# A recurrence whose gate products move behind the next group's second product

## The chip, the cores and the metric

One Trainium2 chip, one of its cores. The metric is device time in microseconds of one execution of the whole program. Engines are named as in the profile: PE (TensorE, matmuls; PEld its weight loads), DVE (VectorE), ACT (ScalarE), POOL (GpSimd), and SP (SyncE), which issues nearly all DMAs in order.

## What is computed

One inference step of a two-layer decoder: a recurrent layer (Hawk/Griffin RG-LRU) and a forgetting-attention layer, for a prompt of 2048 tokens and for 8 x 8 sample tokens, with a model width of 1024. The change lies in the recurrent layer alone:

```
def rg_lru(u, h0, w_ga, b_ga, w_gx, b_gx, lam):
    ub = uf.reshape(B, T, N_RNN_BLOCKS, RNN_BLOCK)
    r = sigmoid(einsum('btnc,ncd->btnd', ub, w_ga) + b_ga)
    i = sigmoid(einsum('btnc,ncd->btnd', ub, w_gx) + b_gx)
    log_a = -RGLRU_C * r * softplus(-lam)
    a = exp(log_a)
    inp = sqrt(-expm1(2.0 * log_a)) * (i * uf)
    # h[t] = a[t] * h[t-1] + inp[t]

def recurrent_mixer(x, h0, conv_buf, w_in, conv_w, conv_b, w_ga, b_ga, w_gx, b_gx, lam, w_out):
    z = x @ w_in
    u, g = z[..., :D_RNN], z[..., D_RNN:]
    u, new_buf = causal_conv(u, conv_buf, conv_w, conv_b)
    h, h_last = rg_lru(u, h0, w_ga, b_ga, w_gx, b_gx, lam)
    return (h * silu(g)) @ w_out, h_last, new_buf
```

Two products per channel block, u and g, come from the input; u is convolved over time, goes through two small gate products (128 x 128 per block), gives the decay a and the input of a scan over time, and the scan's result, times silu(g), is multiplied by w_out.

## The kernel before

**Tiling.** The tokens run through the recurrent layer in two chunks of 1024 (chunk 0 has the 64 sample tokens as well), here called phase 0 and phase 1 of the recurrence. In each, `phase_a1` (L588) loops over the eight channel blocks n (128 channels each) and, within a block, over three groups of tokens: 320, 384 and 384 columns in phase 0 (the 64 sample columns are in the first), 384, 384 and 256 in phase 1. A group is written (n, gi) below. Every product is taken in three float32r parts (`mm3`, L387 to L389: high x high, high x low, low x high), so u and g of a group are 24 matmuls each and its two gates 3 each.

**One group.** `u` is the first product (24 matmuls into a PSUM tile). ACT copies it to `up` (L710). `front` (L592) forms the convolution `uc` in four DVE passes (L597, three times L599), its rounded copy `uh` on POOL (L106) and the rest `ul` on DVE (L111). `gates` (L617) multiplies uh and ul by the block's gate weights gh and gl into two PSUM tiles and takes tanh on ACT (`tr`, `ti`, L624). `g` is the second product, and `tg` its silu in two steps (ACT tanh L724, DVE L725). `decay` (L629) makes `a`, a second tanh of tr and a square `w` on ACT (L635 to L637), then ti and w on DVE (L638, L639). When all three groups of a block are through, `decayed` (L671) takes one square root over the block (L681, with a table load before and after it); for the last block the root is taken group by group (L677). `scan` (L642) multiplies ti by w on POOL, scans over time on DVE (L653, the eight sample rows by short scans L649), carries the last state to the next group on POOL (`hcar`), multiplies by tg on POOL, rounds the result on ACT (`oh`) and DVE (`ol`), and stores both by DMA (L662, L663).

**Software pipelining.** A group's gates and decay are not done in its own turn but in the next group's: `pend` holds the group before. In the kernel before, a turn issues u, then the gates of pend, then g, then the decay of pend, then tg, then one waiting scan. The last group's gates follow the loop (L743).

**What sets the order.** The program is recorded in the order of the code, and a scheduler then places the instructions of each engine by that order's priority and by a timeline of its own, so that small pieces can be moved. Each engine then runs its list strictly in the order placed. Buffers: four PSUM tiles for u, g and y (`mm`), two for gates and transposes (`tp`); uc has three buffers, uh and ul two, tr two, ti and a four, w two, tg five.

**Around the phase.** `then()` and `begin()` (L740, L742) open `phase_a2` (L767), which multiplies oh and ol, read back from DRAM as `ohT` and `olT` (L781), by w_out into `y`; its first two token tiles are loaded in two halves (blocks 0 to 3 and 4 to 7). w_out comes in eight pieces through the staging buffer `wst` (L487, three buffers) and is split on ACT and DVE into high and low parts (`wh`/`wl`, then `woh4` to `woh7`). After phase_a2 of phase 0 come the attention layer's projections and part of the decoding for the samples, then phase 1, and then the rest.

Of the kernel before, what the change touches and what calls it, by code (L numbers as in the profile page):

```python
# [90 lines left out]
def tile_hawk_fox(  # L91
# [496 lines left out]
    def phase_a1(s, xs, a0, covered, feed, wk, out, then, begin, beside):  # L588
# [96 lines left out]
        for n in range(KB):  # L685
            W = feed.take()
            gst = wk.tile([P, 2, P], F32, name="gst", tag="gst")
            S.dma_start(gst[:, 0, :], a_w_ga[0, n])
            asked = S.dma_start(gst[:, 1, :], a_w_gx[0, n])
            gh = wk.tile([P, 2, P], F32R, name="gh", tag="gh", bufs=2)  # L690
            gl = wk.tile([P, 2, P], F32R, name="gl", tag="gl", bufs=2)
            cp(G, gh[:, :, :], gst[:, :, :])
            tt(G, gl[:, :, :], gst[:, :, :], f(gh[:, :, :]), ALU.subtract)
            for gi, (c0, C) in enumerate(s.groups):
                while covered < c0 + C:
                    covered = next(a0)
                so = sm if c0 == 0 else 0
                tn = C - so
                xh, xl = xs[gi]
                rh, rl = (lambda k: xh[:, k, :]), (lambda k: xl[:, k, :])  # L700
                up = wk.tile([P, 3 + mh], F32, name="up", tag="up", bufs=2)
                cp(G, up[:, 0:3], halo[:, n, :])
                ups = mmp("u")
                mm3(ups[:, :C], W.h(0, P), W.l(0, P), rh, rl, KB)
                us = None
                if so:
                    us = wk.tile([P, DB, 3 + DS], F32, name="us", tag="us")
                    cp(G, us[:, :, 0:3], gv[:, n, 11:35].rearrange("p (b j) -> p b j", b=DB))
                    A.copy(us[:, :, 3:], ups[:, :sm].rearrange("p (b q) -> p b q", b=DB))
                A.copy(up[:, 3:3 + tn], ups[:, so:C])  # L710
                uc, uh, ul = front(n, c0, C, ups, us, up, W)
                if so and n == 0:
                    decays()
                if beside and gi < 2:
                    with tc.issue_after(asked.ins):
                        beside.pop(0)()
                if pend:
                    trti = gated()
                gps = mmp("g")
                mm3(gps[:, :C], W.h(P, 2 * P), W.l(P, 2 * P), rh, rl, KB)  # L720
                if pend:
                    decayed(*trti)
                tg = wk.tile([P, mh], F32, name="tg", tag="tg", bufs=5)
                A.activation(tg[:, :C], gps[:, :C], AF.Tanh, scale=0.5)  # L724
                V.scalar_tensor_tensor(tg[:, :C], tg[:, :C], 1.0, gps[:, :C], op0=ALU.add, op1=ALU.mult)  # L725
                if scans:
                    scan(*scans.pop(0))
                pend = (n, c0, C, uc, uh, ul, tg, gh, gl)
                if n == KB - 1:
                    if gi == 0:  # L730
                        out.fetch()
                        out.fetch()
                    else:
                        out.split(min(gi, 2))
                elif gi == 0:
                    feed.fetch()
                    feed.fetch()
                else:
                    feed.split()
# [1275 lines left out]
```

## Time and profile before

| what | us |
|---|---|
| median of 3 runs | 2928.73 (2923.12 to 2936.70) |
| profiled execution | 2919.81 |
| its span | 2918.1 |
| PE busy | 2747.1 (94% of the span) |
| DVE busy | 1828.1 (63%) |
| ACT busy | 1267.6 (43%) |
| POOL busy | 1098.0 (38%) |
| first to last product of u, phase 0 | 32.8 to about 259 |
| phase 1 ends with the store of the last group | about 1126 |

Times in rows of the trace are microseconds from the start of the span. A row of the timeline reads: start, duration, engine, line, operation, tile written <- tiles read, shape, count, and in brackets how long the engine stood idle before it and what ended that. A row of a stretch reads: from:to, length, then busy time and instructions of PE, PEld, DVE, ACT and POOL, the granted clock of PE as a share, the share of the DMA engines and GB/s. A row of the waits reads: engine, tile and line that waited <- engine, tile and line waited for, microseconds in total, times, the longest. Matmuls overlap: the shown duration of one is longer than the step from one start to the next.

### The profile page before, as it was taken

What the parts mean: (1) busy time and instruction counts of PE and PEld (TensorE: products, weight loads), DVE (VectorE), ACT (ScalarE), POOL (GpSimd) and SP (SyncE); (2) the same over time, 40 slices, a digit from 0 to 9 for tenths busy, and PEclk for the clock granted to TensorE, in tenths of its full rate; (3) what the DMA queues carried; (4) which work ended last, traced back from release to release, by engine and by line L of the source; (5) the groups of instructions that cost most, each with busy time, mean ns of one, the idle gap of its engine ahead of it and who ended that gap; (6) DMA issues with size and microseconds to landing.
All of it is one profiled execution on the core that took longest, in us unless ns stands there. A gap on an engine that the chain in (4) does not pass through costs nothing.

```text
span 2918.1 us, 59421 instructions
## 1 busy us (share of the span) xinstructions
PE 2747.1 (94%) x21086; PEld 2224.8 (76%) x21086; DVE 1828.1 (63%) x3971; ACT 1267.6 (43%) x2874; POOL 1098.0 (38%) x1207
## 2 busy tenths in 40 slices
PE   5998999999998999999999999999999999999998
PEld 5997789988898997887888766565666665666787
DVE  7877457244256775676565676767677766655465
ACT  4656342222234665533334345444444544455221
POOL 1654110000003652100001265756565655659554
PEclk9999999999999999999999999999999999999999
DMA  4224536789745536689999978778788777862454
GB/s 127 80 86 125 169 124 188 203 243 300 224 142 177 178 107 191 215 303 325 341 314 333 338 261 293 239 255 277 253 271 269 255 259 240 284 222 61 131 184 131
DMA packets 484789, 636.03 MB, mean 218 GB/s; under 512 B 100888, under 2 KB 293145, under 8 KB 477276
## 3 DMA queue, kind: packets, MB, share of 16 engines
q1 hardware_dynamic: 484204, 630.13, 66.6%
q8 instruction: 167, 2.74, 0.4%
q0 software_dynamic: 288, 2.10, 0.3%
q14 instruction: 130, 1.06, 0.1%
HBM read 512.78 MB, written 133.85 MB: 222 GB/s over the span
## 4 chain that ended last, share of the span: by engine, by line
PE 55%; DMA 9%; DVE 7%; ACT 4%; SPq 3%; issue 2%; POOL 1%; DVEq 0%; ACTq 0%; POOLq 0%
PE ops L1675 8%; PE st L1651 5%; PE sx L1438 4%; PE st L1652 4%; PE dS L1202 3%; PE dO L1290 3%; PE y L389 3%; PE y L387 3%; PE y L388 3%; DMA raw<-in_cache_k_dram 2%; PE kv L387 2%; PE kv L389 2%; PE kv L388 2%; PE qg L387 2%; PE qg L389 2%
## 5 line engine op out<-in xcount | busy, mean ns | idle before, releaser
L1218 DVE STREAM_TRANSPOSE ktr<-raw 128x1024 f32<-128x1024 f32 x256 | 308.0, 1225 | 97.6 <-DMA raw<-in_cache_k_dram 73.5
L1440 DVE TENSOR_REDUCE mxs<-sx 128x1 f32<-128x512 f32 x384 | 253.8, 680 | 157.6 <-PE sx L1438 156.8
L387 PE MATMUL kv<-wh,xh 128*128 128x256 f32 (+3 forms) x1088 | 307.7, 287 | 3.0 <-ACT wh L432 1.7
L389 PE MATMUL kv<-wh,xl 128*128 128x256 f32 (+3 forms) x1088 | 307.1, 284 | 0.4 <-DMA xl<-xld 0.4
L388 PE MATMUL kv<-wl,xh 128*128 128x256 f32 (+3 forms) x1088 | 306.6, 284 | 0.4 <-DVE wl L433 0.3
L433 DVE SCALAR_TENSOR_TENSOR wl<-wst,gv,wh 128x256 fp32r<-128x256 f32 (+1 forms) x384 | 171.1, 494 | 130.7 <-ACT wh L432 130.6
L432 ACT ACTIVATE wh<-wst,gv 128x256 fp32r<-128x256 f32 (+1 forms) x384 | 164.4, 499 | 200.4 <-DMA wst<-in_b_w_in_dram 83.0
L389 PE MATMUL qg<-xh,wl 128*128 128x384 f32 (+2 forms) x640 | 227.5, 357 | 2.2 <-DVE wl L433 2.2
L387 PE MATMUL qg<-xh,wh 128*128 128x512 f32 (+2 forms) x640 | 229.2, 359 | 0.0
L388 PE MATMUL qg<-xl,wh 128*128 128x512 f32 (+2 forms) x640 | 228.1, 358 | 0.0
L387 PEld LDWEIGHTS kv<-wh,xh 128*128 128x128 f32 (+1 forms) x1088 | 201.1, 186 | 8.7 <-issue 3.7
L389 PEld LDWEIGHTS kv<-wh,xl 128*128 128x128 f32 (+1 forms) x1088 | 202.3, 186 | 3.1 <-issue 2.4
L388 PEld LDWEIGHTS kv<-wl,xh 128*128 128x128 f32 (+1 forms) x1088 | 201.5, 186 | 4.1 <-issue 2.5
L1166 POOL TENSOR_TENSOR qw<-qb,amask 128x128 f32<-128x128 f32 x64 | 26.7, 422 | 459.9 <-PE dS L1202 197.7
L1662 ACT ACTIVATE attl<-st 128x512 f32<-128x512 f32 (+3 forms) x236 | 120.5, 524 | 129.2 <-PE st L1652 61.4
L1444 DVE CUSTOM_DVE_ANT_0 sx<-sx,maskb 128x128 f32<-128x128 f32 (+3 forms) x256 | 123.1, 488 | 70.9 <-PE sx L1438 64.9
L1662 ACT ACTIVATE attw<-st 128x512 f32<-128x512 f32 (+3 forms) x224 | 118.0, 550 | 102.4 <-PE st L1652 68.1
L1290 PE MATMUL dO<-raw,sc 128*32 128x256 f32 x2048 | 141.9, 398 | 20.7 <-DMA raw<-in_cache_v_dram 19.9
L111 POOL TENSOR_TENSOR atth<-atth,attl 128x512 f32<-128x512 f32 (+3 forms) x119 | 128.1, 1079 | 65.9 <-ACT attl L1662 47.7
L111 POOL TENSOR_TENSOR atth<-atth,attw 128x512 f32<-128x512 f32 (+3 forms) x116 | 132.3, 1141 | 38.9 <-ACT attw L1662 22.1
L1202 PE MATMUL dS<-ktr,qw 128*32 128x128 f32 x4096 | 129.8, 282 | 14.4 <-DVE ktr L1218 13.5
L925 ACT COPY kf<-kv 128x256 f32<-128x256 f32 (+1 forms) x136 | 49.0, 366 | 217.1 <-PE kv L389 152.7
(359 smaller groups left out, 7651.8 us busy)
## 6 DMA issues: line engine op xcount, KB each, us to landing
raw<-in_cache_k_dram SPq DMA_DIRECT2D x512, 256.0 KB
raw<-in_cache_v_dram SPq DMA_DIRECT2D x512, 256.0 KB
wst<-in_w_kv_dram SPq DMA_DIRECT2D x48, 512.0 KB
wst<-in_b_w_in_dram SPq DMA_DIRECT2D x48, 512.0 KB
xt<-in_x_prompt_dram SPq DMA_DIRECT2D x32, 512.0 KB
wst<-in_a_w_in_dram SPq DMA_DIRECT2D x64, 256.0 KB
out_dram<-kf SPq DMA_DIRECT2D x128, 128.0 KB
cb<-cd SPq DMA_DIRECT2D x14, 1024.0 KB
```

The costliest lines, as they stand in the source:

```text
L111: eng.tensor_tensor(out, a, b, op=op)
L387: T.matmul(ps, lh(k), rh(k), start=(k == 0), stop=False)
L388: T.matmul(ps, lh(k), rl(k), start=False, stop=False)
L389: end = T.matmul(ps, ll(k), rh(k), start=False, stop=(k == nk - 1))
L432: A.activation(wh[:, k, :], st[:, k, :], AF.Copy, scale=gk)
L433: V.scalar_tensor_tensor(wl[:, k, :], st[:, k, :], gk, f(wh[:, k, :]), op0=ALU.mult, op1=ALU.subtract)
L1202: return T.matmul(sp[c * 32:(c + 1) * 32, h * P:(h + 1) * P], qw[:, pp * 2 + h // 2, h % 2 * 2 + x, :], kt[:, :, :, i0:i0 + 8], start=(x = ...
L1218: behind("V", V.transpose(t.kts[pp][:, n], raw[:, :, pp * 256:(pp + 1) * 256]).ins)
L1290: return T.matmul(op[c:c + 32, :256], t.sc[:, i // 4, m, a * 4:(a + 1) * 4, :].rearrange("p h q -> p (h q)"), raw[:, m, a * 256:(a + 1) * ...
L1440: r = V.reduce_max(mx[:, j, ck:ck + 1], ps[:, :w], axis=AX.X)
L1662: pair.append((k, lo, p, A.activation(p[:, lo:], ps[:, lo:], AF.Exp)))
L1675: return T.matmul(ops[r * HD:(r + 1) * HD, a0 * P:], vvs[h % 2][:, k, :], p[:, :].rearrange("p (a r c) -> p a r c", a=2, r=2)[:, a0:, r, : ...
```

## The change

In a turn, the gates of the group before are issued behind the second product g instead of ahead of it, and its decay behind tg instead of ahead of it:

```
@@ -714,15 +714,14 @@
                 if beside and gi < 2:
                     with tc.issue_after(asked.ins):
                         beside.pop(0)()
-                if pend:
-                    trti = gated()
                 gps = mmp("g")
                 mm3(gps[:, :C], W.h(P, 2 * P), W.l(P, 2 * P), rh, rl, KB)
-                if pend:
-                    decayed(*trti)
+                trti = gated() if pend else None
                 tg = wk.tile([P, mh], F32, name="tg", tag="tg", bufs=5)
                 A.activation(tg[:, :C], gps[:, :C], AF.Tanh, scale=0.5)
                 V.scalar_tensor_tensor(tg[:, :C], tg[:, :C], 1.0, gps[:, :C], op0=ALU.add, op1=ALU.mult)
+                if pend:
+                    decayed(*trti)
                 if scans:
                     scan(*scans.pop(0))
                 pend = (n, c0, C, uc, uh, ul, tg, gh, gl)
```

What the scheduler makes of it is seen in the order of each engine. Tiles carry running numbers there, so that a group can be followed; the lines of the kernel after are one lower from L722 on (L724 and L725 of before are L721 and L722).

**PE in the middle of phase 0**, at the turn of a group (n, 1): u_2206 is its first product, the uh_2128 in the gates is that of the group before, (n, 0). Before:

```order
L388 MATMUL u_2206<-xl_201,wh_2075 128x384
L389 MATMUL u_2206<-xh_200,wl_2076 128x384
L387 MATMUL gate_2244<-uh_2128,gh_2082 128x320
L388 MATMUL gate_2244<-ul_2129,gh_2082 128x320
L389 MATMUL gate_2244<-uh_2128,gl_2083 128x320
L387 MATMUL gate_2249<-uh_2128,gh_2082 128x320
L388 MATMUL gate_2249<-ul_2129,gh_2082 128x320
L389 MATMUL gate_2249<-uh_2128,gl_2083 128x320
L387 MATMUL g_2254<-xh_200,wh_1977 128x384
```

After:

```order
L387 MATMUL g_2242<-xh_200,wh_2075 128x384
L388 MATMUL g_2242<-xl_201,wh_2075 128x384
L389 MATMUL g_2242<-xh_200,wl_2076 128x384
L387 MATMUL gate_2269<-uh_2128,gh_2082 128x320
L388 MATMUL gate_2269<-ul_2129,gh_2082 128x320
L389 MATMUL gate_2269<-uh_2128,gl_2083 128x320
L387 MATMUL gate_2274<-uh_2128,gh_2082 128x320
L388 MATMUL gate_2274<-ul_2129,gh_2082 128x320
L389 MATMUL gate_2274<-uh_2128,gl_2083 128x320
L387 MATMUL u_2305<-xh_202,wh_1977 128x384
```

The six gate products stood between u and g of the next group and stand behind its g now, right ahead of the u of the group after. In other turns of before the scheduler had put a few products of g ahead of the gates, up to nine; after, all 24 always are.

**DVE at the same turn**, from the first pass of the convolution of (n, 1), uc_2232, to its ul_2239. w_1958 (before) and w_1961 (after) hold the scans of the block before, ti_2243 and ti_2268 belong to the decay of (n, 0). Before:

```order
L597 TENSOR_SCALAR uc_2232<-up_2204,gv_114 128x384
L638 SCALAR_TENSOR_TENSOR ti_2243<-ti_2243,uc_2117 128x320
L599 SCALAR_TENSOR_TENSOR uc_2232<-up_2204,gv_114,uc_2232 128x384
L653 SCALAR_TENSOR_TENSOR w_1958<-a_2169,hcar_122,ti_2133 128x384
L111 TENSOR_TENSOR ol_2193<-tg_1854,oh_2192 128x320
L599 SCALAR_TENSOR_TENSOR uc_2232<-up_2204,gv_114,uc_2232 128x384
L639 SCALAR_TENSOR_TENSOR w_2280<-w_2280,tr_2242 128x320
L111 TENSOR_TENSOR ol_2294<-tg_1964,oh_2293 128x384
L599 SCALAR_TENSOR_TENSOR uc_2232<-up_2204,gv_114,uc_2232 128x384
L111 TENSOR_TENSOR ol_2392<-tg_2062,oh_2391 128x384
L725 SCALAR_TENSOR_TENSOR tg_2286<-tg_2286,g_2254 128x384
L111 TENSOR_TENSOR ul_2239<-uc_2232,uh_2238 128x384
```

After:

```order
L597 TENSOR_SCALAR uc_2232<-up_2204,gv_114 128x384
L649 SCALAR_TENSOR_TENSOR w_1961<-a_1960,gv_114,ti_1946 128x8 x8
L653 SCALAR_TENSOR_TENSOR w_1961<-a_1960,hcar_122,ti_1946 128x256
L599 SCALAR_TENSOR_TENSOR uc_2232<-up_2204,gv_114,uc_2232 128x384 x2
L653 SCALAR_TENSOR_TENSOR w_1961<-a_2059,hcar_122,ti_2045 128x384
L599 SCALAR_TENSOR_TENSOR uc_2232<-up_2204,gv_114,uc_2232 128x384
L722 SCALAR_TENSOR_TENSOR tg_2279<-tg_2279,g_2242 128x384
L653 SCALAR_TENSOR_TENSOR w_1961<-a_2172,hcar_122,ti_2158 128x384
L111 TENSOR_TENSOR ol_2193<-tg_1847,oh_2192 128x320
L638 SCALAR_TENSOR_TENSOR ti_2268<-ti_2268,uc_2117 128x320
L111 TENSOR_TENSOR ul_2239<-uc_2232,uh_2238 128x384
```

The first pass of uc moved ahead of the scans of the block before (the short scans and the first two long ones stood ahead of it); the third long scan, two ol and the two decay steps of (n, 0), ti and w, stood ahead of the last pass of uc and stand behind it.

**PE at the end of phase 0**: gate_3093 and gate_3098 are the gates of the last group (7, 2), y_3148 the first product of phase_a2. Before:

```order
L387 MATMUL g_2995<-xh_202,wh_2716 128x384
L388 MATMUL g_2995<-xl_203,wh_2716 128x384
L389 MATMUL g_2995<-xh_202,wl_2717 128x384
L387 MATMUL gate_3093<-uh_2979,gh_2723 128x384
L387 MATMUL gate_3098<-uh_2979,gh_2723 128x384
L388 MATMUL gate_3093<-ul_2980,gh_2723 128x384
L389 MATMUL gate_3093<-uh_2979,gl_2724 128x384
L388 MATMUL gate_3098<-ul_2980,gh_2723 128x384
L389 MATMUL gate_3098<-uh_2979,gl_2724 128x384
L387 MATMUL y_3148<-wh_2939,ohT_3073 64x512
```

After:

```order
L387 MATMUL y_3148<-wh_3040,ohT_3073 64x512
L388 MATMUL y_3148<-wl_3041,ohT_3073 64x512
L389 MATMUL y_3148<-wh_3040,olT_3074 64x512
L387 MATMUL gate_3093<-uh_2979,gh_2723 128x384
L387 MATMUL gate_3098<-uh_2979,gh_2723 128x384
L388 MATMUL gate_3093<-ul_2980,gh_2723 128x384
L389 MATMUL gate_3093<-uh_2979,gl_2724 128x384
L388 MATMUL gate_3098<-ul_2980,gh_2723 128x384
L389 MATMUL gate_3098<-uh_2979,gl_2724 128x384
L387 MATMUL y_3193<-wh_2939,ohT_3081 128x512
```

The gates of (7, 1) follow the last g there, then come the first 12 products of y_3148, and the gates of (7, 2) stand behind these. In phase 1 it is 25 products of y. The other queues move in keeping: on ACT the tanh of g stands ahead of the decay of the group before, and in phase 1 the splits woh5, woh6 and woh7 stand ahead of the last group's tr, where woh4 alone did; in phase 0 woh5 moved behind the last square root. On SP the stores of oh and ol of a group follow each other, and in phase 0 the first ohT loads stand behind the stores of block 6 instead of behind those of (7, 0) and a piece of w_out. Behind the first products of the attention layer the order of all engines is as before but for a few rows.

More of the change, by code (lines that the diff above doesn't have):

```diff
@@ L716, in phase_a1 @@
                         beside.pop(0)()
-                if pend:
-                    trti = gated()
                 gps = mmp("g")
                 mm3(gps[:, :C], W.h(P, 2 * P), W.l(P, 2 * P), rh, rl, KB)
-                if pend:
-                    decayed(*trti)
+                trti = gated() if pend else None
                 tg = wk.tile([P, mh], F32, name="tg", tag="tg", bufs=5)
@@ L725, in phase_a1 @@
                 V.scalar_tensor_tensor(tg[:, :C], tg[:, :C], 1.0, gps[:, :C], op0=ALU.add, op1=ALU.mult)
+                if pend:
+                    decayed(*trti)
                 if scans:
```

## Prediction

> **What bounds the kernel now.** The page first: one core, and TensorE is busy for most of the span. Then the busy time by stretch, for a steady part of each of the two recurrence phases.
>
> ```profile
> span 2918.1 us, 59421 instructions
> PE 2747.1 (94%) x21086; PEld 2224.8 (76%) x21086; DVE 1828.1 (63%) x3971; ACT 1267.6 (43%) x2874; POOL 1098.0 (38%) x1207
> ...
> 97.00:237.00 140.00, 134.23 (x802) 132.64 (x803) 112.26 (x216) 88.50 (x152) 85.02 (x123) 1.00 0.26 83
> 940.00:1100.00 160.00, 154.91 (x973) 152.05 (x973) 120.64 (x190) 103.43 (x176) 89.70 (x140) 1.00 0.45 149
> ```
>
> TensorE (PE) is the engine with the least slack in both stretches: 134.23 of 140 us and 154.91 of 160, against 112 to 121 for VectorE (DVE). What a change of order can win here is what PE waits for, so the next view is who PE waited for, in the first phase (30 to 280 us) and in the second (880 to 1120 us).
>
> ```profile
> PE gate L387 <- POOL uh L106: 11.7, 8, 2.7
> PE y L387 <- DMA ohT<-oh: 3.2, 1, 3.2
> ...
> PE gate L387 <- POOL uh L106: 5.0, 7, 1.2
> ```
>
> The gate products wait for uh, the rounded copy of the group's convolution, which GpSimd (POOL) writes: 16.7 us in 15 waits. The timeline shows them at fixed places. These four rows are the first and the last steady one of each phase:
>
> ```profile
> 97.46 0.62 PE L387 MATMUL gate<-uh,gh 128*128 128x384 f32 x2 [1.95 <-POOL uh L106]
> 236.82 0.63 PE L387 MATMUL gate<-uh,gh 128*128 128x384 f32 x2 [0.97 <-POOL uh L106]
> ...
> 940.06 0.62 PE L387 MATMUL gate<-uh,gh 128*128 128x384 f32 x2 [1.23 <-POOL uh L106]
> 1099.71 0.45 PE L387 MATMUL gate<-uh,gh 128*128 128x384 f32 x1 [0.51 <-POOL uh L106]
> ```
>
> The idle figure understates a wait, since the matmuls right behind it also run at a longer step. So I measure the loss against the steps that undisturbed rows give, start to start:
>
> ```profile
> 250.27 0.34 PE L387 MATMUL u<-xh,wh 128*128 128x384 f32 x1
> ...
> 254.47 0.31 PE L387 MATMUL gate<-uh,gh 128*128 128x320 f32 x1
> ...
> 255.35 0.34 PE L387 MATMUL g<-xh,wh 128*128 128x384 f32 x1
> ...
> 1074.75 0.28 PE L387 MATMUL g<-xh,wh 128*128 128x256 f32 x1
> ...
> 1077.58 0.33 PE L387 MATMUL u<-xh,wh 128*128 128x384 f32 x1
> ```
>
> 24 products of 384 columns lie between 250.27 and 254.47, so 0.175 us each; six of 320 between 254.47 and 255.35, 0.147 each; 24 of 256 between 1074.75 and 1077.58, 0.118 each. One block n of phase 0 has 108 products of 384 and 54 of 320, 26.84 us. From 97.46 to 236.82 there are five blocks in 139.36 us; the order of before has nine products of g ahead of the first of these gates and none ahead of the last, which takes 1.6 off, so the floor is 5 x 26.84 - 1.6 = 132.6 and **6.8 us** are lost, and 1.95 ahead of 97.46: 8.7. Phase 1 has 108 products of 384 and 54 of 256 in a block, 25.27 us; six blocks take 159.65 from 940.06 to 1099.71, so **8.0** are lost, and 1.23 ahead of them: 9.3. **18.0 us** are what the steady waits cost.
>
> **The change part by part.** No instruction is added or removed: 24 groups in each phase keep their six gate products, five ACT steps and two DVE steps of decay. What moves is where they stand. PE's order becomes u, g, gates of the group before, without the gates inside or ahead of g. So the front of a group (up copy, four uc passes, uh, ul) has one more g, 24 x 0.175 = 4.2 us, before its gates are due. SP's queue is passed too: stores of oh and ol go out in pairs, and at the two ends of phase the loads of ohT change their place.
>
> *Is 4.2 us enough?* The waits fall on group (n,1), whose front stands behind the square root and the scans of block n-1. Those hang on gates (n-1,2), which the change puts one g later as well, so this chain moves by the same 4.0 to 4.2 us. Here it is as it ran, for one block of each phase:
>
> ```profile
> 190.64 0.31 PE L387 MATMUL g<-xh,wh 128*128 128x320 f32 x1
> ...
> 194.61 1.12 ACT L681 ACTIVATE w<-w 128x1088 f32<-128x1088 f32 x1
> ...
> 200.60 1.62 DVE L653 TENSOR_TENSOR_SCAN w<-a,hcar,ti 128x384 f32<-128x384 f32 x1 [0.31 <-POOL hcar L106]
> ...
> 204.21 1.00 DVE L653 TENSOR_TENSOR_SCAN w<-a,hcar,ti 128x384 f32<-128x384 f32 x1
> ...
> 206.05 1.29 DVE L639 SCALAR_TENSOR_TENSOR w<-w,tr 128x320 f32<-128x320 f32 x1
> ...
> 208.43 0.76 POOL L106 TENSOR_SCALAR uh<-uc 128x384 fp32r<-128x384 f32 x1 [1.43 <-ACT up L710]
> ...
> 209.22 0.56 DVE L111 TENSOR_TENSOR ul<-uc,uh 128x384 fp32r<-128x384 f32 x1
> ...
> 1029.67 0.34 PE L389 MATMUL g<-xh,wl 128*128 128x384 f32 x1
> ...
> 1033.22 1.06 ACT L681 ACTIVATE w<-w 128x1024 f32<-128x1024 f32 x1
> ...
> 1045.71 0.63 POOL L106 TENSOR_SCALAR uh<-uc 128x384 fp32r<-128x384 f32 x1 [1.55 <-DVE uc L599]
> ```
>
> In phase 0 gates (n-1,2) end at 190.64; the root ends 5.1 later at 195.73; uh ends at 209.19, 13.5 after the root, ul at 209.78, 14.1 after it. In the new order PE has u 4.2, g 4.2, gates (n,0) 0.88, u 4.2, g 4.2 = 17.7 us between the end of gates (n-1,2) and gates (n,1), so these start 12.6 after the root. With the chain as long as now, uh would still be 0.9 late. But the new DVE order lets the last uc pass overtake: gone from ahead of it are the third scan (1.00), w (1.29), ti and two ol (about 0.5 each), 3.8 in all, and tg's wait no longer stands ahead of the scans. I add up DVE's rows in the new order from the root on: up 0.5, uc 0.45, eight short scans 1.7, scan 0.73, two uc 1.2, scan 1.62, uc 0.6: 6.9, with the POOL product and uh behind it 8.7; and tg 0.5, scan 1.0, ol, ti, ul 0.5 each: ul at 9.9. In phase 1 the gates (n-1,2) end at 1029.67, the root 4.6 later, uh at 1046.34, 12.1 after it; the new order gives 4.2 + 4.2 + 1.05 + 2.8 + 2.8 = 15.1, so 10.5 after the root; the same sum, without short scans, gives uh at 7.7 and ul at 9.1. Both are in time by 1.4 to 4 us. **I take all 18.0.** The ends: 0 where the chain stays as long as it is, 18.0 where it is short.
>
> *What is late next?* Between blocks nothing: PE itself, at 26.84 and 25.27 us a block. The tanh of g on ACT no longer waits between decay steps; the root and two table loads per block are as before. POOL and DVE have the same work in 4 to 5% less time; DVE now works 112 of 140 us. The decay steps' place behind tanh I cost at nothing: with a table load they take ACT the 4.0 us from 190.64 to 194.61, and PE's next u and g, 8.4 us, hide them; without that cover each group would lose up to 4 us.
>
> *End of phase 0.* Counted from the start of the last u, 259.56:
>
> ```profile
> 259.56 0.34 PE L387 MATMUL u<-xh,wh 128*128 128x384 f32 x1
> ...
> 274.66 0.38 SPq L487 DMA_DIRECT2D wst<-in_a_w_out_dram  x1
> 275.13 0.42 SPq L781 DMA_DIRECT2D ohT<-oh  x1
> ...
> 277.44 0.59 ACT L624 ACTIVATE tr<-gate,hb_ga 128x384 f32<-128x384 f32 x1
> ...
> 279.79 0.69 PE L387 MATMUL y<-wh,ohT 128*64 128x512 f32 x1 [3.18 <-DMA ohT<-oh]
> ...
> 284.59 1.04 PE L758 MATMUL stp<-ident,st_s 128*32 128x128 f32 x8
> ...
> 287.32 0.52 ACT L677 ACTIVATE w<-w 128x384 f32<-128x384 f32 x1 [0.64 <-DVE w L639]
> ```
>
> Now the last gates stall, then the first 12 y products wait 3.18 us for ohT, whose load left SP behind a weight tile that was waiting for its buffer, and run at a step of 0.43 against 0.23 later; all are done at 284.59, 25.0 in. In the new order these 12 y stand ahead of the last gates, so a wait for their load is new there: behind it stand the last gates, and behind those ACT's last tr. The load itself stands behind the stores of block 6 alone. The last group's ul hangs on the chain through ACT and DVE and comes at 17, by the same adding up (16.0 now, at 275.60). So the last gates end near 17.7 with the 12 y behind them already: 7.3 won. Given back: the split of woh5 now stands behind ACT's last root. From tr at 277.44 to that root's end at 287.84 are 10.4 us with 1.7 of the split and a wait in them, so woh5 comes at about 17.7 + 8.7 = 26.4 with its end, the products of the second half reach it about 3 earlier, and wait. And tile 0's products end 20 ahead of the last one instead of 13, which covers 1.1 of idle at 306. Net **5 won**; ends -2 (nothing won, the two late splits waited for) and +10 (no wait for woh5 either).
>
> *End of phase 1.* From the start of the last u, 1096.22:
>
> ```profile
> 1096.22 0.28 PE L387 MATMUL u<-xh,wh 128*128 128x256 f32 x1
> ...
> 1112.31 0.47 ACT L624 ACTIVATE tr<-gate,hb_ga 128x256 f32<-128x256 f32 x1
> ...
> 1117.36 1.05 ACT L104 CAST woh<-wst 128x1024 fp32r<-128x1024 f32 x1 [2.78 <-DMA wst<-in_a_w_out_dram]
> ...
> 1125.62 0.42 DVE L111 TENSOR_TENSOR ol<-tg,oh 128x256 fp32r<-128x256 f32 x1 [1.22 <-ACT oh L104]
> ...
> 1129.38 0.85 SPq L781 DMA_DIRECT2D ohT<-oh  x1
> ...
> 1135.81 0.77 PE L387 MATMUL y<-wh,ohT 128*128 128x512 f32 x1 [4.97 <-DMA ohT<-oh]
> ```
>
> Here tile 2's load is the end of a chain: last ol at 1126.04, SP's five weight loads, ohT at 1129.38, PE at 1135.81, 39.6 in. The new order keeps that queue on SP. On ACT it puts woh5, woh6 and woh7 ahead of the last tr, where now only woh4 stands; the last tr comes at about 21 in, against 16.1, but without the 2.78 us that ACT then stood for woh5's tile. Added up, the last ol ends at 29.6, now 29.8: no gain and no loss, PE only waits longer in one piece. About 1 of the 9.3 above lies behind 1096.22 and so is not won: **-1**. Ends: -8 (three splits each wait as woh5 did, 2.78) and +4 (the last ol comes 4 earlier).
>
> The start, before 97 us, I leave at 0, ends -2 and +2. **Sum: 18.0 + 5 - 1 = 22 us.** Against the profiled execution, 2919.81 us, of which the span is 2918.10, this gives 2898. That execution is 8.9 below the median of 2928.73 us, so against the median **2907 us**.
>
> **A rule to weigh.** DVE's scan of 384 took 1.62 us at 200.60, beside a POOL product, and 1.00 at 204.21. The Trainium skill, GPSIMD Engine Reference, section 1 Specifications, says that GpSimd shares its SBUF interfaces with VectorE and contends with Vector instructions that have two SBUF inputs, which speaks against this change, since it packs the same DVE and POOL work into less time. The trace agrees: the slow scan ran beside POOL, the fast one mostly did not. By that rule every scan of the chain would be priced like the slow row, ul would come about 0.6 us later than summed, and the gain would stay 18; only if w and ol slow down too does it shrink.
>
> **The rivals.** (1) *The waits move along with the chain.* The change then does not do what it says: uh is 0.9 late in phase 0 and 1.6 in phase 1 as computed above with the chain unshortened, as now. 0 + 5 - 1 = 4 us, 2925. For it: the chain starts later by just what the front wins. Against: 3.8 us of DVE steps leave it. (2) *The ends of phase give it back.* The steady 18 come, but the y products and weight splits that now stand ahead of the last gates and the last tr each wait for their DMA: 18 - 2 - 8 = 8 us, 2921. For it: ACT stood 2.78 for one tile in phase 1. (3) *Slower: contention on the boundary.* The three scans, with a POOL product each between them, run like the 1.62 us row and hand over late; ul then ends last. It decides from a chain of over 12.6 us (phase 0) and 10.5 (phase 1) after the root, and loses against now once it is 1.3 longer still, the loss of a block today. At 2.7 us over the due time in 14 blocks it costs 38 against 18 now, so 20 more, less the 4 of the two ends: 16 slower, 2945. Against: the sum above stands 1.4 to 2.7 below the limit for ul even with one slow scan. This is how the rule above would act here.
>
> **How the numbers follow.** About 0.5%, 14.6 us, is what a measurement of this kernel can tell from no change. Forecast 0.64, with its own range from 18 - 6 = 12 to 18 + 10 + 4 + 2 = 34 us won, 2895 to 2917; rival (2) 0.17; rival (1) 0.13; rival (3) 0.06. Faster by over 0.5%: the forecast, less its lower edge, and nothing else: 0.62. Within: 0.32. Slower: 0.06. The range takes in the forecast and both small gains and leaves out rival (3): 2894 to 2926.
>
> **What would show it.** In the changed profile the gate products should wait for uh and ul for under 3 us in both phases, and six blocks of phase 1 should take 152 us. PE should run 12 y of phase 0 ahead of the last gates, and wait again for woh5; the last ol of phase 1 should stand 29 to 31 us behind the start of its last u. The prediction is wrong if gates still wait 10 us or more, above all for ul, or if PE stands over 8 us longer than now in the 40 us behind a last u.

## The result, and the profile after

Over eight runs each, the changed kernel took 2912.39 us and the kernel before 2925.93 (medians); the ratio is 0.995, with a 95% interval of 0.9935 to 0.9966. So 13.5 us were won where 22 were forecast: just inside the forecast's own range (12 to 34), and a little under the 14.6 that the prediction took as the least to be told from no change. The head of the changed kernel's page:

```profile
span 2911.8 us, 59422 instructions
...
PE 2748.2 (94%) x21086; PEld 2226.9 (76%) x21086; DVE 1857.9 (64%) x3971; ACT 1263.9 (43%) x2874; POOL 1107.4 (38%) x1207
```

Its stretch of five blocks of phase 0, columns as in the prediction's first fence:

```profile
97.00:237.00 140.00, 137.41 (x821) 135.53 (x820) 126.43 (x218) 87.19 (x151) 87.64 (x124) 1.00 0.26 84
```

And its PE waits, the gates' rows, in phase 0 (20 to 320 us; the first two) and in phase 1 (870 to 1180):

```profile
PE gate L388 <- DVE ul L111: 1.9, 4, 0.6
...
PE gate L387 <- POOL uh L106: 0.7, 1, 0.7
...
PE gate L387 <- POOL uh L106: 1.8, 1, 1.8
PE gate L388 <- DVE ul L111: 0.9, 1, 0.9
```

PE worked 137.41 of the 140 us instead of 134.23. The waits of the gates for uh and ul fell from 18.8 us (16.7 for uh, 0.9 and 1.2 for ul) to 5.3 in the two phases together, 2.6 and 2.7; under 3 in each had been forecast. What is left in phase 0 is new: it names ul (DVE), where before it named uh (POOL).

To see where the time went, the same product is looked up in both traces; these are starts of rows of the timeline.

| start of | before, us | after, us | earlier by |
|---|---|---|---|
| first u of phase 0 | 32.80 | 32.23 | 0.57 |
| u of (7,2), phase 0 | 259.56 | 255.23 | 4.33 |
| last y of phase 0 | 392.25 | 386.15 | 6.10 |
| first u of phase 1 | 876.55 | 870.55 | 6.00 |
| u of (7,2), phase 1 | 1096.22 | 1081.71 | 14.51 |
| last y of phase 1 | 1209.60 | 1196.43 | 13.17 |
| last product of the program | 2908.89 | 2901.94 | 6.95 |

Phase 1 wins 8.5 up to its last u and loses 1.3 at its end; phase 0 wins 3.8 and 1.8, both counted from the phase's first u. Behind the last y of phase 1 this pair of traces loses 6.2 us again, in the decoding, whose order the change leaves alone. That is spread between executions: one program run twice (the kernel before, and the run below in which only the decay's place in the code was changed) took 1699.3 and 1705.2 us for the same stretch. The eight runs (13.5) agree with the 13.2 at 1196 us, not with the 6.3 between the two spans.

The steady part of phase 0, by blocks (from the u of one group (n,0) to the next, in us):

| kernel | n=0 | 1 | 2 | 3 | 4 | 5 | 6 |
|---|---|---|---|---|---|---|---|
| before | 33.73 | 34.70 | 28.77 | 27.97 | 28.11 | 27.99 | 28.11 |
| after | 34.68 | 32.41 | 28.66 | 26.92 | 27.61 | 27.65 | 27.65 |
| weight splits on DVE | 36.04 | 32.38 | 26.84 | 26.90 | 26.84 | 26.90 | 26.84 |
| weight splits on POOL | 38.83 | 32.41 | 31.14 | 26.90 | 28.12 | 28.38 | 28.15 |

The floor worked out ahead, 26.84, is right, as the third row shows; the changed kernel stays 0.8 above it in three of the five blocks from n=2 on, and 1.8 in n=2. The timeline of the changed kernel shows why: DVE, POOL and PE around the gates of a block's last group (a group (n-1,2); its gates now stand behind the next block's first g).

```profile
185.89 1.22 DVE L111 TENSOR_TENSOR wl<-wst,wh 128x1024 fp32r<-128x1024 f32 x1
187.46 2.40 POOL L111 TENSOR_TENSOR wl<-wst,wh 128x1024 fp32r<-128x1024 f32 x1
187.52 2.76 DVE L111 TENSOR_TENSOR ul<-uc,uh 128x384 fp32r<-128x384 f32 x1 [0.41 <-POOL uh L106]
...
189.56 0.34 PE L387 MATMUL gate<-uh,gh 128*128 128x384 f32 x1
190.33 0.44 PE L388 MATMUL gate<-ul,gh 128*128 128x384 f32 x1 [0.43 <-DVE ul L111]
```

The second row is the low half of a weight piece on POOL, 2.40 us; ul starts 0.06 behind it on DVE, takes 2.76 us and ends 0.42 behind POOL's end. PE stands 0.43 us for it, and as the matmuls behind it run at a longer step, the gates take 1.74 us from 189.56 to the next u at 191.30, 0.7 more than six products of 0.175. The same group of instructions in both kernels, 60 to 275 us (ul of 384 columns: count, busy, mean ns of one), before and after:

```profile
L111 DVE TENSOR_TENSOR ul<-uc,uh 128x384 fp32r<-128x384 f32 x14 | 7.8, 555 | 2.5 <-POOL uh L106 2.5
```

```profile
L111 DVE TENSOR_TENSOR ul<-uc,uh 128x384 fp32r<-128x384 f32 x15 | 17.9, 1191 | 2.8 <-POOL uh L106 2.8
```

555 ns have become 1191 on the mean. In the kernel before, POOL's piece, in four blocks of six, fell into a time in which DVE had only tg to do (next fence, before: POOL's row, then DVE's), which reads g from PSUM and took the same 0.56 us as elsewhere:

```profile
187.24 2.40 POOL L111 TENSOR_TENSOR wl<-wst,wh 128x1024 fp32r<-128x1024 f32 x1 [1.95 <-ACT wh L104]
...
187.58 0.56 DVE L725 SCALAR_TENSOR_TENSOR tg<-tg,g 128x384 f32<-128x384 f32 x1 [0.28 <-ACT tg L724]
```

### The profile page after: what moved, and what is told of

It is laid out like the page before. It is cut to its first block, busy times and chain, and to the rows that moved or that the text cites. A ratio compares the mean times of both kernels' runs of the same rounds, so it can differ in the third digit from the quotient of the medians.

```text
span 2911.8 us, 59422 instructions
## 1 busy us (share of the span) xinstructions
PE 2748.2 (94%) x21086; PEld 2226.9 (76%) x21086; DVE 1857.9 (64%) x3971; ACT 1263.9 (43%) x2874; POOL 1107.4 (38%) x1207
## 4 chain that ended last, share of the span: by engine, by line
PE 53%; DMA 12%; DVE 6%; SPq 4%; ACT 3%; issue 2%; POOL 1%; DVEq 0%; ACTq 0%; POOLq 0%
PE ops L1674 8%; PE st L1650 5%; PE sx L1437 4%; PE st L1651 3%; PE dO L1289 3%; PE dS L1201 3%; DMA raw<-in_cache_k_dram 3%; PE y L387 3%; PE y L389 3%; PE y L388 3%; DMA raw<-in_cache_v_dram 2%; PE qg L389 2%; PE qg L387 2%; PE qg L388 2%; PE kv L387 2%
```

## The experiments

Theory A: the gates' place wins the steady waits, and what is left in phase 0 is POOL's share of the weight split, which holds DVE and so ul of (n-1,2) up. Theory B: the chain through the square root moves along with the gates, so that uh or ul are late whatever POOL does. Theory C: the decay's place matters, not the gates'.

**Splits on DVE, and on POOL.** The low halves of the recurrence's weight pieces go to DVE and POOL by turns; one letter changes that:

```
-    w_l = Turns(nc, "VG")
+    w_l = Turns(nc, "V")      # first run
+    w_l = Turns(nc, "G")      # second run
```

> Changed kernel, with the low half of every weight piece of the recurrence taken on DVE; in the changed kernel every second piece goes to POOL, and a DVE step beside it took 2.76 us instead of 0.55. Theory A (POOL's split holds DVE up, and with it ul of the last group of a block): no ul of 384 columns in phase 0 takes over 1.5 us between blocks, the gates wait under 0.5 us from 90 to 255 us, five blocks of u take 134 to 136 us instead of 138.5, and the last u of phase 0 starts 7 to 9 us before that of the kernel before instead of 4.3. Theory B (the chain through the square root moved along with the gates, and the split is by the way): the gates go on waiting for ul at the same places, and the last u starts 4.3 us earlier, plus or minus 0.7, or less, as DVE has 8 more splits. Phase 1 under both: its 24 groups win 8.5 us, plus or minus 1.

> Changed kernel, with the low half of every weight piece of the recurrence taken on POOL (the opposite of the run before). Theory A: two collisions of about 2.2 us a block instead of one; the gates wait over 4 us in phase 0 (now 2.6) and the last u of phase 0 starts at most 2.5 us before that of the kernel before, or later than it. Theory B: DVE has 1.2 us a block less to do and nothing else changes; the last u starts 4 to 6 us earlier.

The stretch of five blocks with the splits on DVE, and ul of 384 columns there (60 to 275 us):

```profile
97.00:237.00 140.00, 140.00 (x846) 140.00 (x845) 124.68 (x230) 90.54 (x158) 77.81 (x120) 1.00 0.28 89
```

```profile
L111 DVE TENSOR_TENSOR ul<-uc,uh 128x384 fp32r<-128x384 f32 x16 | 9.7, 604 | 3.6 <-POOL uh L106 3.6
```

With the splits on POOL, the same group of ul, and what PE waited for from 90 to 260 us:

```profile
L111 DVE TENSOR_TENSOR ul<-uc,uh 128x384 fp32r<-128x384 f32 x14 | 19.4, 1384 | 1.1 <-POOL uh L106 1.1
```

```profile
PE gate L388 <- DVE ul L111: 5.6, 4, 2.3
```

With the splits on DVE, PE does not stand at all for 140 us, though DVE has five more splits to do in them; ul takes 604 ns on the mean, and five blocks take 134.32 us (the sum of n=2 to 6 above). The last u started 6.7 us earlier than before, 7 to 9 having been expected, because the first block took 36.04; from the end of that block it is 8.9. Phase 1 won 10.0 us up to its last u, more than the expected 8.5 plus or minus 1. With all of them on POOL ul takes 1384 ns on the mean, the gates wait 5.6 us for it, and the last u starts 1.5 us later than before; counted from the end of the first block it is 0.5 earlier, where the changed kernel wins 4.7. The expected second collision a block did not come: one ul a block took 2.70 to 2.77 us, five rows in all. Theory A holds, and B falls: with the order of the chain unchanged the waits are gone.

**One half of the change at a time.** Only the gates moved (the decay stays ahead of tg; its edit against the changed kernel follows), and only the decay moved (gates ahead of g, decay behind tg):

```
                 mm3(gps[:, :C], W.h(P, 2 * P), W.l(P, 2 * P), rh, rl, KB)
-                trti = gated() if pend else None
+                if pend:
+                    decayed(*gated())
                 tg = wk.tile([P, mh], F32, name="tg", tag="tg", bufs=5)
...
-                if pend:
-                    decayed(*trti)
```

> Only the gate products move behind g; the decay steps stay ahead of the tanh of g, where they were. Theory A (the place of the gates is what wins; the decay's place only takes DVE steps off the chain): the gates still wait less than in the kernel before (16.7 us for uh), but more than in the changed one (2.5): phase 0 wins 1 to 4 us up to the last u, phase 1 5 to 8.5. Theory C (the decay's place is what matters, since the 3.8 us of DVE steps leave the chain by it): no gain in the steady blocks, under 1.5 us in either phase.

> Only the decay steps move behind the tanh of g; the gate products stay ahead of g. Theory A: the gates go on waiting, over 12 us for uh and ul, and the last u of either phase starts within 2 us of the kernel before, counted from the phase's start. Theory C: the waits fall to under 8 us, and the phases win over half of what the changed kernel wins (4.3 and 8.5).

The scheduler gives the first, row for row on all five queues, the order of the changed kernel, and the second that of the kernel before. So the decay's place in the code does nothing, theory C falls, and the two traces are repeats: the waits above those of the changed kernel that had been expected of the first could not come, and its phase 1 won 9.3 us, not 5 to 8.5. From the end of the first block to u of (7,0) they took 170.82 us (170.90 in the changed kernel) and 175.54 (175.65 before): such stretches repeat to 0.1 us. The first block does not: 38.65 us with only the gates moved against 34.68 in the changed kernel.

**The end of phase 0.** From the start of the last u to the last y took 132.69 us before and 130.92 after. The changed kernel's order of the end took 130.76 and 129.57 in two more runs, so a difference of about 1 us here says nothing. Four runs change what stands ahead of the last gates. In the first the last turn keeps the old order:

```
+                old = n == KB - 1 and gi == len(s.groups) - 1
+                trti = gated() if pend and old else None
                 gps = mmp("g")
...
```

> Changed kernel, but the very last turn of each phase, group (7,2), keeps the old order: gates of (7,1) ahead of the last g. On PE only two products of y then stand ahead of the last gates of phase 0, instead of 12. The changed kernel won 1.8 us from the start of the last u to the last y of phase 0, and lost 1.3 in phase 1. Theory D (the 12 y and their wait for ohT, which stand ahead of the last gates, give the gain of the end back): phase 0 wins 4 to 7 us there, and the last gates start under 17.5 us behind the start of the last u (19.3 in the changed kernel). Theory E (the last gates are late whatever stands ahead of them, since up of (7,2) is copied on ACT only behind the square root of (7,0), and this order keeps that): the last gates start 18 us or more behind the last u's start, and phase 0 wins under 3. Steady blocks under both: as in the changed kernel to 0.3 us a block.

In the second, the square roots of (7,0) and (7,1) are one instruction behind the loop:

```
-            if n == KB - 1:
+            if n == KB - 1 and c0 == s.groups[-1][0]:
                 A.activation(w, w, AF.Sqrt, scale=0.25)
...
         then()
+        w = ws[KB - 1][:, 0:s.groups[-1][0]]
+        A.activation(w, w, AF.Sqrt, scale=0.25)
...
```

> Changed kernel, with the square roots of (7,0) and (7,1) taken together behind the loop: ACT then copies up of (7,2) ahead of them, and has one root and two table loads less at each end; woh5 stands ahead of the last root on ACT. The 12 y ahead of the last gates stay. Theory E: up of (7,2) is copied under 2 us after the last u's products end (6 in the changed kernel), ul of (7,2) ends under 17 us behind the start of the last u instead of 19.2, the wait of y for woh5 (2.9) goes under 1, and phase 0 wins 4 to 8 us from the last u to the last y instead of 1.8; phase 1 is between -1.3 and +3. Theory D: ul comes earlier, but the 12 y still wait over 3 us for ohT and hold the gates past 18 us; phase 0 wins under 3.

With the old last turn the stretch took 135.03 us (a wait of 5.9 for ACT is new) and the last gates started at 18.0: D missed, and E's two limits were met. With the late roots it took 132.85, though up of (7,2) was copied 4.5 us behind the last u's products instead of 6 (under 2 had been expected) and its ul ended 14.5 us behind the start of the last u instead of 19.2: E missed, and D was near, with a wait of 3.3 for ohT and gates that started at 17.9, not past 18. The scan of (7,0) had to wait for the joint root, its store came 9 us later on SP and the loads of the second half of the blocks 10, and PE stood 4.1 us for them. Phase 1's end lost 2.5 us against the kernel before, where -1.3 to +3 had been expected. So neither D nor E alone sets the end's length; as the late roots made a wait of their own, the second run does not rule out that E has a part. Put together with the splits on DVE, the late roots also cost in the whole:

> The late roots together with the low halves of the weight pieces on DVE. If the two causes are separate, their gains add: phase 0 to the last u as in the run with the splits on DVE (176.7 us from the first block's end to the last u would be 184.1, against 193.0 before), the ends as in the run with the late roots, phase 1's blocks 25.2 to 25.4 us each. The whole: 18 to 25 us below the kernel before, 5 to 11 below the changed one (13.5 below before). If DVE or ACT become the bound at the ends, it stays within 4 us of the changed kernel.

It came to 0.9966 of the kernel before (0.9952 to 0.9979), 9.2 us less by the medians where 18 to 25 had been expected, and no better than the changed kernel: steady blocks at 26.85 to 26.89, but 133.96 us at the end of phase 0 and 119.59 (before 113.38) at that of phase 1. The gains do not add.

In the last two of this kind the order was forced, with the splits on DVE: the low halves of w_out from the third piece on behind the last ul on DVE, with the second piece's split moved behind the loop in both phases, and then also oh of (7,0) behind ti of (7,1) on ACT:

```
+                if i >= 2 and self.last_ul is not None:
+                    tc.add_manual_dep(low.ins, self.last_ul.name, ORDER)
...
+            if n == KB - 1 and c0 == 0:
+                tc.add_manual_dep(cast.ins, out.last_ti.name, ORDER)
...
-                        out.split(min(gi, 2))
+                        out.split(1)
```

> The run with the weights' low halves on DVE, and at the end of each phase the low halves of the third and later pieces of w_out held behind ul of (7,2) on DVE (they stood ahead of it, 2.4 us). In phase 1 woh6 and woh7 also come behind the last tr on ACT. In the run with the splits on DVE, ul of (7,2) ended 18.2 us behind the start of the last u, the gates of (7,2) started at 18.25, ready for ul and for their PSUM tile (tr of (7,1)) at the same time. If ul holds the end: ul ends under 16.5, and the last u to the last y of phase 0 falls from 128.6 by 1.5 us or more. If tr on ACT holds it as well (it waits behind the cast of oh of (7,0), which waits for POOL): ul comes as early, the gates start at 18.0 to 18.4 all the same, and the stretch stays within 0.7 us. Phase 1, last u to last y: 115.6 there; 113 to 116.

> The run before, with the cast of oh of (7,0) held behind tr and ti of (7,1) on ACT as well. If ul and tr held the last gates together: both are there by 16.5 us, the gates start when the 12 y are through, 17.2 to 17.6 behind the last u's start, ACT's last root ends 1.5 us earlier or more, and the last u to the last y of phase 0 falls to 126 to 127.5. If the wait of y for ohT is what holds the end, nothing changes: 128 to 129. The steady blocks as in the run with the splits on DVE. The whole: 2 us or less below that run.

The last gates did start earlier, 15.6 and 16.5 us behind the start of the last u instead of 18.25, and ACT split woh5 3.7 us earlier in the second. But the stretch took 130.42 and 131.07, against 128.58 and 128.38 in the two runs without forcing. The end of phase 1 took 118.20 and 116.68 us, 113 to 116 having been expected, and the whole of the second was 13.2 us below the kernel before (0.9955, 0.9938 to 0.9972): the forcing costs. The rows of PE that waited in the second of them, behind its start of the last u (251.61):

```profile
263.74 0.69 PE L387 MATMUL y<-wh,ohT 128*64 128x512 f32 x1 [2.49 <-DMA ohT<-oh]
270.56 0.50 PE L387 MATMUL y<-woh,ohT 128*128 128x512 f32 x1 [0.56 <-DVE tg L731]
276.96 0.68 PE L387 MATMUL y<-woh,ohT 128*64 128x512 f32 x2 [0.40 <-ACT woh L104]
278.66 0.45 PE L388 MATMUL y<-wol,ohT 128*64 128x512 f32 x1 [1.02 <-DVE wol L501]
283.12 0.45 PE L388 MATMUL y<-wol,ohT 128*64 128x512 f32 x1 [1.24 <-DVE wol L501]
287.56 0.69 PE L389 MATMUL y<-wh,olT 128*64 128x512 f32 x1 [3.06 <-DMA olT<-ol]
```

And the four us behind the last of these, as a stretch:

```profile
288.00:292.00 4.00, 4.00 (x13) 2.17 (x12) 0.00 (x0) 0.34 (x1) 0.00 (x0) 0.63 0.24 77
```

In place of the wait of 3.1 for the last gates there are waits for wol (1.02 and 1.24 us, against one of 0.58) and for olT (3.06), and behind the last of them the granted clock is 0.63 on the mean of four us. In both runs ul ended under 16.5 us, as expected, but none of the lengths expected for the stretch came: neither ul and tr nor y's ohT alone holds the end. A reading that fits, and that is not shown, is that several chains (last gates, splits of w_out, stores of (7,0) and their loads) end close together, and when one is shortened, the next takes over. What sets the end, and which order would be best there, stays open.

**The splits on DVE, timed.**

> The run with the weights' low halves on DVE once more, timed: by its trace phase 0 wins 4.2 us more than the changed kernel between the first block's end and the last u, and phase 1 wins 0.5 to 1.2 more; with the end of phase 0 (2.3 more) that makes 16 to 22 us below the kernel before, against 13.5 for the changed kernel. If the first run's end of phase 0 was chance, 14 to 19.

The ratio to the kernel before was 0.9931 (0.9911 to 0.9950): 2901.52 against 2923.80 us, 22 us less by the medians and 20 by the ratio, where 16 to 22 had been expected. Its interval overlaps that of the changed kernel (0.9935 to 0.9966), and the two were not timed against each other, so the step from the one to the other is shown in the trace's stretches alone.

**The start.** Only the first block of phase 0 in the old order, on the changed kernel and on the run with the splits on DVE:

```
+                old = n == 0 and s.i == 0
+                trti = gated() if pend and old else None
                 gps = mmp("g")
...
```

> Changed kernel, but the three turns of the first block of phase 0 keep the old order (gates ahead of g). In that block, from the first u to the first u of block 1, two traces of the old order took 33.7 and 34.5 us, four of the new order 34.7, 37.5, 37.6 and 38.7. Theory S (the new order itself makes the first block longer, since the tiles of tokens that are still being transposed leave PE idle there and its granted clock falls to 0.50): the block takes 33.5 to 35 us here, and no stretch of it from 60 to 70 us runs at a clock under 0.9. Theory N (chance, whatever the order): 34 to 39, and more likely over 36. Blocks 1 to 6 as in the changed kernel to 0.3 us each, the second at 32.4 or 34.7.

> The same on top of the run with the weights' low halves on DVE (whose first block took 36.0 and 36.7 us, and whose blocks 2 to 6 stood at 26.85 to 26.89). Theory S: the first block takes 33.5 to 35 us, blocks 2 to 6 stay at 26.8 to 26.9, and the whole is 1 to 3 us below that run: 18 to 24 us below the kernel before. Theory N: first block 34 to 39, the whole within 2 us of that run. If the gates of the first block in the old order collide with the splits on DVE, the second block takes over 33.5 us.

The block took 35.94 and 35.52 us: longer than the 33.5 to 35 of theory S, whose clock did stay up, and inside the 34 to 39 of N, though not over 36. Of all traces, four with the old order there took 33.7 to 35.9 (mean 34.9), ten with the new one 34.1 to 38.8 (mean 36.6). Six of those ten show a granted clock under 0.9 between 60 and 70 us, none of the four. This is the stretch 63 to 66 us in the changed kernel and, below, in the run with the gates alone, which has the same order:

```profile
63.00:66.00 3.00, 3.00 (x23) 2.99 (x22) 0.13 (x1) 0.10 (x1) 0.00 (x0) 1.00 0.00 0
```

```profile
63.00:66.00 3.00, 2.48 (x9) 2.48 (x10) 0.69 (x1) 0.47 (x1) 0.00 (x0) 0.50 0.00 0
```

At a clock of 0.50 nine products fit where 23 did. In the four blocks of the new order whose clock stayed up, three took 34.1 to 35.7 us, as in the old order; the fourth, 38.8 with the splits on POOL, had begun at 29.7, at least 1.6 us ahead of all others. So the new order seems to cost 1 to 2 us there, by chance of the clock; that is an indication and no proof. In the whole, the old start on top of the splits on DVE came to 0.9928 (0.9909 to 0.9947) of the kernel before, its interval much the same as that of the splits on DVE alone; by the medians it is 15.3 us less, where theory S had 18 to 24.

On the changed kernel, the old start showed something else. Blocks 2 and 3 stood at the floor (26.85 and 26.89, where 28.66 and 26.92 to 0.3 had been expected), although ul took 2.75 us beside POOL there too: it ended 1.1 us before its product in block 2, 0.3 in block 3, and after its due time from block 4 on, which took 27.5 to 27.7. The square roots of that run tell why:

```profile
84.93 1.11 ACT L681 ACTIVATE w<-w 128x1088 f32<-128x1088 f32 x1
...
112.57 1.11 ACT L681 ACTIVATE w<-w 128x1088 f32<-128x1088 f32 x1 [0.71 <-DVE w L639]
...
140.20 1.11 ACT L681 ACTIVATE w<-w 128x1088 f32<-128x1088 f32 x1 [1.54 <-DVE w L639]
...
167.84 1.11 ACT L681 ACTIVATE w<-w 128x1088 f32<-128x1088 f32 x1 [1.70 <-DVE w L639]
```

They stand 27.63 or 27.64 us apart from the first one on, also in the two blocks in which PE took 26.85 and 26.89 and no gate waited. With POOL's split beside ul it is thus no longer PE that sets the pace of the blocks, but the chain through DVE, POOL and ACT, 0.8 us a block slower than PE's products; it eats the gates' margin, and then PE stands for the difference. With the splits on DVE the roots stand 26.8 to 26.9 apart, PE's own pace, and with all of them on POOL about 28.3. Which steps of the chain make up its 27.6 us was not taken apart.

## Why the prediction was right, and where it was off

The sign, the place and the range were right, the sum was 8.5 too large. Every term fell short or was right, none made up for another. Term by term, from the table of starts:

- *Steady waits of phase 1, 9.3 (some 1 of it counted at the end):* 8.5 measured, of which 0.9 came in the first block, whose length differed by 1.2 between two runs of the order of before. The six blocks forecast at 152 us took 152.82, between the same gates at 934.56 and 1087.38. The margin of 1.4 for ul was not there: it ended 10.55 us behind the root instead of 9.1, 0.2 ahead of its product in five blocks and late in the sixth, where PE stood 0.86. That it was mostly in time is luck: the sum was 1.4 short.
- *Steady waits of phase 0, 8.7:* this is the step that failed. 3.8 came. Block 1 gave 2.3, where the 1.95 ahead of 97.46 had been seen; blocks 2 to 6 gave 2.5 instead of 6.8 (140.95 to 138.49 us); the first block lost 1.0. The answer to "what is late next", nothing between blocks, was wrong twice. First, the sum stopped at the group (n,1). The gates of the next one, (n,2), are due 7.1 us (u and g of 320 columns) behind the first u of the next block, and its ul met POOL's split, as shown above. Second, the margin for (n,1) itself was used up. Its ul ended 11.2 us behind the root instead of 9.9, the eight short scans, beside POOL, having taken 2.80 us instead of 1.7. And the gates were due 11.0 behind the root instead of 12.6, since the root ended 6.6 us behind the gates (n-1,2), which ended at 163.66, instead of 5.1; ACT had waited 1.69 for w on DVE. So ul, due with 2.7 to spare, ended as PE came to it (rows of ACT, DVE and PE, changed kernel):

```profile
169.19 1.11 ACT L681 ACTIVATE w<-w 128x1088 f32<-128x1088 f32 x1 [1.69 <-DVE w L639]
...
171.40 2.80 DVE L649 TENSOR_TENSOR_SCAN w<-a,gv,ti 128x8 f32<-128x8 f32 x8
...
180.92 0.54 DVE L111 TENSOR_TENSOR ul<-uc,uh 128x384 fp32r<-128x384 f32 x1
...
181.51 0.45 PE L388 MATMUL gate<-ul,gh 128*128 128x384 f32 x1
```

With the splits on DVE the root ended 5.0 behind the gates again, and ul had 1.7 to spare: of the lost 2.7 us of margin some 1.6 go back to POOL's split, too.

- *"DVE now works 112 of 140 us":* in the same stretch it works 126.43. No step is new, the same ones take longer: in this stretch ul of 384 columns 8.2 us more (14.3 instead of 6.1) and the short scans 5.5 (14.0 instead of 8.5). The rule weighed there, of the Trainium skill (GPSIMD Engine Reference, section 1 Specifications), named this contention. The trace agrees with it, in more than the prediction gave it: 0.6 us for slow scans was allowed, and one collision took 2.2 (2.76 against 0.56).
- *End of phase 0, 5:* 1.8 measured, 2.3 in the repeat against its own (133.09 and 130.76). The 12 y stood ahead of the last gates, as forecast, and waited for ohT (3.38); the last gates started at 19.3 and were through at 20.6, not 17.7, since up of (7,2) stood on ACT behind the square root of (7,0); woh5 ended at 30.1 instead of 26.4, and y waited 2.90 for it (rows of ACT and PE):

```profile
265.69 0.46 ACT L710 COPY up<-u 128x384 f32<-128x384 f32 x1
268.43 0.69 PE L387 MATMUL y<-wh,ohT 128*64 128x512 f32 x1 [3.38 <-DMA ohT<-oh]
...
274.51 0.82 PE L387 MATMUL gate<-uh,gh 128*128 128x384 f32 x2 [0.70 <-ACT tr L624]
285.36 0.68 PE L387 MATMUL y<-woh,ohT 128*64 128x512 f32 x2 [2.90 <-ACT woh L104]
```

```profile
268.00:272.00 4.00, 3.57 (x9) 1.81 (x10) 4.00 (x11) 2.74 (x4) 3.14 (x3) 0.50 1.06 224
```

The last row, a stretch, is a price that I left out: behind such a wait the granted clock is 0.50, so y runs at a step of 0.43 for 5 us. That the late gates set the end is not shown; the forced orders speak against it. What the late gates and the late woh5 each cost stays open.
- *End of phase 1, -1:* -1.3 measured. The last ol ends 31.3 us behind the last u's start, 29.6 having been summed up, just over the 29 to 31 forecast, and PE then waits for tile 2 as before, later by 1.9 us in the stretch:

```profile
1112.59 0.42 DVE L111 TENSOR_TENSOR ol<-tg,oh 128x256 fp32r<-128x256 f32 x1 [1.60 <-ACT oh L104]
...
1123.19 0.47 PE L387 MATMUL y<-wh,ohT 128*128 128x512 f32 x1 [3.80 <-DMA ohT<-oh]
```

- *The decay's place, costed at nothing:* right, and for a simpler reason: the order that the scheduler makes doesn't depend on it.

Of the rivals, the first (waits move along) came true in part, at another group and by another cause; the second in part at both ends (1.8 and -1.3, where it had -2 and -8). The third named the right mechanism, contention at the block boundary; it slowed the eight short scans, but what came late was ul of (n-1,2), and PE lost 0.7 to 0.9 us a block where 2.7 had been priced.

## What to carry to other kernels

When a wait goes, work out the due time of every group in the pattern, not only of the one that waited: here the next group had less slack than the one that was freed. Work out the pace of the other engines' chain as well: a chain 0.8 us a block slower than PE eats any margin in a few blocks. Before packing DVE and POOL more tightly, list the long POOL operations and look which DVE steps that read only SBUF can fall beside them. And code moved inside a scheduled program may move nothing: compare the orders of each half before crediting it.

## What the runs showed of the hardware

A DVE step of 384 columns with two SBUF inputs that started beside a POOL step of 1024 stood until that had ended (2.75 or 2.76 us instead of 0.55, in 13 rows of ul in three runs, each ending 0.41 or 0.42 us behind POOL's end). Beside a shorter POOL step it was the same on a smaller scale: in phase 1 ul took 1.09 us beside tg's 0.74 and again ended 0.41 behind it. A step with one input in PSUM took its 0.56. Two tensors from SBUF are not needed for it: in the changed kernel uc's first pass (L597) of 256 columns, which reads one, took 2.65 us beside POOL's piece in phase 1, and 0.40 a block earlier, away from it.

And a stall costs more than its idle time where the granted clock falls: it went to 0.50 behind waits of 2.5 to 3.4 us (not behind each of them), and in six of the ten first blocks in the new order behind several short ones. The Trainium skill (TensorE: Matmul & The Clock Gate, Part 1) puts the half clock down to an idle window of about 3.4 us and calls the window free-running. The trace agrees with the second: up to 400 us, all stretches at 0.50 in a run start whole multiples of 3.41 us apart and last one, two or three times 3.41, and the same order met one in one run and missed it in the next (the two rows of 63 to 66 us above). It does not show that PE must stand through the whole of such a window. In the run with the gates alone, PE was busy for 1.59 of the 3.41 us ahead of the fall (two stretches):

```profile
58.81:62.22 3.41, 1.59 (x11) 1.12 (x12) 2.74 (x5) 2.50 (x5) 0.01 (x1) 1.00 0.00 0
62.22:69.05 6.83, 6.16 (x25) 5.71 (x24) 1.38 (x2) 0.58 (x1) 0.00 (x0) 0.50 0.00 0
```
